# Row normalization on one core: the last scale of the first tile is shared between ScalarE and VectorE

## The chip, the cores and the metric

The kernel runs on one core of a Trainium2 chip. The metric is the device time of one execution in microseconds (us); lower is better. The engines that matter here are VectorE (DVE in the profile), ScalarE (ACT), SyncE (SP), which issues the transfers, and the core's sixteen DMA engines, which carry them out. TensorE does nothing.

## The reference

Each of 1024 rows of 4096 fp32 numbers is divided by its Euclidean norm.

```python
def reference(x, axis, eps):            # x: 1024 x 4096, fp32; axis -1; eps 1e-12
    norm = np.sqrt(np.sum(x ** 2, axis=axis, keepdims=True) + eps)
    return (x / norm).astype(np.float32)
```

So 16.78 MB are read and 16.78 MB are written, and each element is squared, summed and scaled once.

## The kernel before

The 1024 rows are cut into two tiles of 512 rows. A tile (`xt`, one `RowGroups` object each) has 128 partitions with R = 4 consecutive rows each, that is 128 x 4 x 4096 fp32 or 8.39 MB, and lies in SBUF whole; both tiles have a buffer of their own. A tile is loaded by one transfer (line 192) and stored by one (line 213), both issued on the SP queue. Both loads are issued ahead of everything else, the first of them moved to the very front of the program. The two stores follow on the same queue, each as soon as all four rows of its tile are scaled. A helper at the end rearranges the closing barrier; the change doesn't touch it.

What is done to a row r of a tile:

- a square with a running sum into `ssq[:, r]`, on ScalarE (`square_act`, line 33) or on VectorE (`square_dve`, line 42); the squares themselves go to a scratch tile that nobody reads
- `norm`: a square root of the sum on ScalarE (line 53), then its reciprocal on VectorE (line 59), into `rstd[:, r]`
- a multiplication of the row by `rstd[:, r]`, in place: on VectorE (`scale`, line 64) or on ScalarE (`scale_act`, line 69)

The order within a tile is written out by hand in the loop at line 197. VectorE squares row 3 while ScalarE squares row 0; VectorE then scales rows 0, 1 and 3 while ScalarE squares rows 1 and 2. Row 2 is the last one whose sum is ready. In the first tile ScalarE scales it (`scale_act`), in the second tile VectorE does (`scale`). Each engine executes its instructions in the order in which they are written; the waits between engines are put in by the framework from what each instruction reads and writes. The store of a tile waits for the scales of all four rows, on both engines.

Of the kernel before, what the change touches and what calls it, by code (L numbers as in the profile page):

```python
# [13 lines left out]
class RowGroups:  # L14
# [50 lines left out]
            out=self.x[:, r], in0=self.x[:, r], scalar1=self.rstd[:, r : r + 1]  # L65
        )

    def scale_act(self, r):
        self.nc.scalar.activation(  # L69
            out=self.x[:, r],  # L70
            in_=self.x[:, r],
            func=ACT_F.Copy,
            scale=self.rstd[:, r : r + 1],
        )


def first_load_to_front(nc, load):

    def move(program):
        blocks = program.main_func.blocks
        entry = blocks[0].instructions
        if any(i.name == load.name for i in entry):
            return
        body = next(
            b.instructions  # L90
            for b in blocks
            if any(i.name == load.name for i in b.instructions)
        )
        at = next(n for n, i in enumerate(body) if i.name == load.name)
        assert not body[at].sync_info.on_wait
        before = next(
            n
            for n, i in enumerate(entry)
            if i.engine == mybir.EngineType.SP and isinstance(i, mybir.InstDrain)
        )  # L100
        entry.insert(before, body.pop(at))

    nc.at_finalize(move)


def one_barrier_behind_last_store(nc, store):

    SP, POOL = mybir.EngineType.SP, mybir.EngineType.Pool

    def waits(i):
        return i.sync_info.on_wait if i.sync_info is not None else []

    def move(program):
        sem = store.sync_info.on_update[0].id
        tail = program.main_func.blocks[-1].instructions  # L120

        def take(which):
            at = next(n for n, i in enumerate(tail) if which(i))
            return tail.pop(at)

        def place(instructions, which):
            at = max(n for n, i in enumerate(tail) if which(i))
            tail[at:at] = instructions

        arrivals = [  # L130
            n
            for n, i in enumerate(tail)
            if i.engine == SP and isinstance(i, mybir.InstDrain)
        ]
        if any(w.id == sem for w in waits(tail[arrivals[-2]])):
            return
        everything = take(
            lambda i: i.engine == SP and any(w.id == sem for w in waits(i))
        )
        place([everything], lambda i: i.engine == SP and isinstance(i, mybir.InstDrain))  # L140
        reset = take(
            lambda i: i.engine == POOL
            and isinstance(i, mybir.InstDrain)
            and i.is_reset_sema
        )
        clear = take(lambda i: i.engine == POOL and isinstance(i, mybir.InstISA))
        place(
            [reset, clear],
            lambda i: i.engine == POOL and isinstance(i, mybir.InstEventSemaphore),
        )  # L150

    nc.at_finalize(move)


@with_exitstack
def kernel(
    ctx: ExitStack,
    tc: tile.TileContext,
    x: bass.AP,
    axis: bass.AP,  # L160
    eps: bass.AP,
    out: bass.AP,
):
    nc = tc.nc
    P = nc.NUM_PARTITIONS

    assert isinstance(axis, int) and axis in (-1, len(x.shape) - 1)
    eps = float(eps)

    x = x.flatten_outer_dims()  # L170
    out_flat = out.flatten_outer_dims()
    N, D = x.shape
    R = 4
    assert N % (P * R) == 0
    n_tiles = N // (P * R)
    x_t = x.rearrange("(t p r) d -> t p (r d)", p=P, r=R)
    out_t = out_flat.rearrange("(t p r) d -> t p (r d)", p=P, r=R)

    io = ctx.enter_context(tc.tile_pool(name="io", bufs=n_tiles))
    scratch_pool = ctx.enter_context(tc.tile_pool(name="scratch", bufs=1))  # L180
    stats = ctx.enter_context(tc.tile_pool(name="stats", bufs=n_tiles))

    eps_t = scratch_pool.tile([P, 1], F32)
    nc.vector.memset(eps_t, eps)  # L184
    sq_act = scratch_pool.tile([P, D], F32)
    sq_dve = scratch_pool.tile([P, D], F32)
    scratch = {"act": sq_act, "dve": sq_dve}

    groups = []
    for i in range(n_tiles):  # L190
        g = RowGroups(nc, io, stats, scratch, D, R, eps_t)
        load = nc.sync.dma_start(out=g.flat(), in_=x_t[i])
        if i == 0:
            first_load_to_front(nc, load.ins)
        groups.append(g)

    for i, g in enumerate(groups):
        g.square_dve(R - 1)
        g.square_act(0)
        g.norm(0)  # L200
        g.scale(0)
        g.square_act(1)
        g.norm(1)
        g.norm(R - 1)
        g.scale(1)
        g.scale(R - 1)
        g.square_act(2)
        g.norm(2)
        if i < n_tiles - 1:
            g.scale_act(2)  # L210
        else:
            g.scale(2)
        store = nc.sync.dma_start(out=out_t[i], in_=g.flat())
    one_barrier_behind_last_store(nc, store.ins)
# [35 lines left out]
```

## Time and profile before

| | |
|---|---|
| median of 5 runs | 82.54 us (82.45 to 82.84) |
| profiled execution: its time | 82.54 us |
| profiled execution: its span in the profile | 80.8 us |
| DMA queue busy, share of 16 engines | 96.8% |
| ScalarE busy | 30.1 us (37%) |
| VectorE busy | 26.2 us (33%) |
| square of a row on ScalarE, 128x4096 | 3.61 us, 6 times |
| square of a row on VectorE, 128x4096 | 4.43 us, 2 times |
| scale of a row on VectorE, 128x4096 | 2.35 us, 7 times |
| scale of a row on ScalarE, 128x4096 | 3.71 us, once |

The span is the time from the first to the last instruction of the program; the execution's time has 1.7 us more around it. "Busy" is the time in which an engine executes an instruction of the program. Transfers are listed in two ways: by their issue on SP, which takes 0.35 us, and by their packets, which the DMA engines move later. A line of the time line reads: start in us, duration in us, engine, line of the kernel, operation, output <- input, shapes, how often, and in brackets the idle time of the engine just before it with what ended that. A line of a window view reads: the window in us and its length, busy time (and number of instructions) of VectorE, ScalarE and GpSimd, the granted clock, the DMA share, and GB/s. In that view a packet's bytes and time are booked whole where the packet starts, so that a short window can show more than the hardware can move; a packet is 65,536 bytes, four rows of one partition.

### The profile page before, as it was taken

The numbers are of one execution on the slowest core, as the hardware profiler recorded it, in microseconds if no ns is written. First come the engines' busy times: TensorE is split into PE (matmuls) and PEld (weight loads), VectorE is DVE, ScalarE is ACT, GpSimd is POOL, SyncE is SP. The second block draws the span as 40 slices with busy tenths as digits, with TensorE's granted clock in tenths as the row PEclk, the third lists the DMA queues.
The fourth block names the chain that finished last, engine by engine and source line by source line (L and its number), as shares of the span: only waits on it lengthen the run. The fifth ranks groups of instructions, "written<-read, shape, count | busy, mean of one in ns | idle before, by whom it ended". The sixth has DMA issues, their size and how long they took to land.

```text
span 80.8 us, 93 instructions
## 1 busy us (share of the span) xinstructions
DVE 26.2 (33%) x20; ACT 30.1 (37%) x23; POOL 0.2 (0%) x4
## 2 busy tenths in 40 slices
DVE  0000000000199599920059986999000000000000
ACT  6000000000199999989459999930000000000000
POOL 0000000000000000000000000000000000000000
DMA  9099999199999199999199993899992999995690
GB/s 487 32 519 519 519 519 454 65 519 519 519 519 454 65 519 519 519 519 454 65 519 519 519 519 162 357 519 519 519 519 97 422 519 519 519 519 227 292 519 0
DMA packets 576, 33.55 MB, mean 416 GB/s; under 512 B 64, under 2 KB 64, under 8 KB 64
## 3 DMA queue, kind: packets, MB, share of 16 engines
q1 hardware_dynamic: 576, 33.55, 96.8%
HBM read 16.78 MB, written 16.78 MB: 416 GB/s over the span
## 4 chain that ended last, share of the span: by engine, by line
DMA 50%; ACT 10%; DVE 9%; issue 0%
DMA xt<-in_x_dram 50%; ACT sq_act L33 9%; DVE xt L64 9%; ACT rstd L53 1%; DVE rstd L59 0%
## 5 line engine op out<-in xcount | busy, mean ns | idle before, releaser
L33 ACT ACTIVATE sq_act<-xt 128x4096 f32<-128x4096 f32 x6 | 21.6, 3608 | 21.9 <-DMA xt<-in_x_dram 21.9
L42 DVE SCALAR_TENSOR_TENSOR sq_dve<-xt 128x4096 f32<-128x4096 f32 x2 | 8.9, 4426 | 26.8 <-DMA xt<-in_x_dram 26.8
L64 DVE TENSOR_SCALAR xt<-xt,rstd 128x4096 f32<-128x4096 f32 x7 | 16.5, 2353 | 0.2
L69 ACT ACTIVATE xt<-xt,rstd 128x4096 f32<-128x4096 f32 x1 | 3.7, 3709 | 0.2 <-DVE rstd L59 0.2
L53 ACT ACTIVATE rstd<-ssq,eps_t 128x1 f32<-128x1 f32 x8 | 2.1, 289 | 0.1
L59 DVE RECIPROCAL rstd<-rstd 128x1 f32<-128x1 f32 x8 | 1.3, 159 | 2.4 <-ACT rstd L53 2.4
L33 ACT ACT_TABLE_LOAD x1 | 1.3, 1283 | 0.8 <-PEq L231 0.8
L53 ACT ACT_TABLE_LOAD x1 | 1.3, 1283 | 0.0
L33 ACT ACTIVATION_READ_ACCUMULATOR sq_act<-xt 128x1 f32 x6 | 1.1, 186 | 0.0
L184 DVE MEMSET eps_t<- 128x1 f32 x1 | 0.1, 59 | 0.8 <-PEq L231 0.8
L42 DVE DVE_READ_ACCUMULATOR sq_dve<-xt 128x1 f32 x2 | 0.2, 82 | 0.0
L231 POOL MEMSET const-uint8-127<- 128x1 uint8 x1 | 0.1, 103 | 0.0
L231 POOL MEMSET const-bfloat16-1.0<- 128x1 bf16 x1 | 0.1, 102 | 0.0
L231 POOL MEMSET const-float32-0.0<- 128x1 f32 x1 | 0.1, 99 | 0.2 <-issue 0.2
L231 POOL MEMSET const-float32-1.0<- 128x1 f32 x1 | 0.1, 99 | 0.0
## 6 DMA issues: line engine op xcount, KB each, us to landing
xt<-in_x_dram SPq DMA_DIRECT2D x2, 31.2
out_dram<-xt SPq DMA_DIRECT2D x2, 22.6
```

Source lines behind the costliest of these rows:

```text
L33: self.nc.scalar.activation(out=sq_a, in_=self.x[:, r], func=ACT_F.Square, accum_out=self.ssq[:, r : r + 1],)
L42: self.nc.vector.scalar_tensor_tensor(out=sq_v, in0=self.x[:, r], scalar=1.0, in1=self.x[:, r], op0=ALU.mult, op1=ALU.mult, accum_out=self ...
L53: self.nc.scalar.activation(out=self.rstd[:, r : r + n], in_=self.ssq[:, r : r + n], func=ACT_F.Sqrt, bias=self.eps_t,)
L59: self.nc.vector.reciprocal(out=self.rstd[:, r : r + n], in_=self.rstd[:, r : r + n])
L64: self.nc.vector.tensor_scalar_mul(out=self.x[:, r], in0=self.x[:, r], scalar1=self.rstd[:, r : r + 1])
L69: self.nc.scalar.activation(out=self.x[:, r], in_=self.x[:, r], func=ACT_F.Copy, scale=self.rstd[:, r : r + 1],)
L184: nc.vector.memset(eps_t, eps)
L231: nc = _bacc.Bacc("TRN2", target_bir_lowering=False, num_devices=1)
```

## The change

In the first tile, the scale of row 2 is cut: columns 0 to 3071 are scaled on ScalarE, columns 3072 to 4095 on VectorE. `scale_act` goes, `scale_by_both` takes its place; VectorE's part is written behind ScalarE's. The second tile is as before.

```diff
-    def scale_act(self, r):
+    def scale_by_both(self, r):
+
+        cut = 3 * self.D // 4
+        rstd = self.rstd[:, r : r + 1]
         self.nc.scalar.activation(
-            out=self.x[:, r],
-            in_=self.x[:, r],
+            out=self.x[:, r, :cut],
+            in_=self.x[:, r, :cut],
             func=ACT_F.Copy,
-            scale=self.rstd[:, r : r + 1],
+            scale=rstd,
+        )
+        self.nc.vector.tensor_scalar_mul(
+            out=self.x[:, r, cut:], in0=self.x[:, r, cut:], scalar1=rstd
         )
...
         g.norm(2)
         if i < n_tiles - 1:
-            g.scale_act(2)
+            g.scale_by_both(2)
         else:
             g.scale(2)
         store = nc.sync.dma_start(out=out_t[i], in_=g.flat())
```

## The prediction, made before the changed kernel was run

> **What bounds the kernel now.** I read the page's slices and queue rows first, because they say whether any compute engine can matter at all.
>
> ```profile
> DVE  0000000000199599920059986999000000000000
> ACT  6000000000199999989459999930000000000000
> DMA  9099999199999199999199993899992999995690
> q1 hardware_dynamic: 576, 33.55, 96.8%
> HBM read 16.78 MB, written 16.78 MB: 416 GB/s over the span
> ```
>
> VectorE and ScalarE are idle for more than half of the span, and the one DMA queue is busy for 96.8% of it on all sixteen engines. The low digits in the DMA row are no pauses: a packet is a block of 64 KB (four rows of 16 KB), booked in the slice in which it starts, so a slice in which no engine happens to start one looks empty. The chain of waits on the page gives DMA 50% and compute 20%, since it follows the last instruction (the second store's issue at 56.6 us) and not the last byte. The transfers themselves end near 79.8 us. So the next view is the time line around the changed instruction, with the queue that carries the store.
>
> ```profile
> 35.29 0.16 DVE L59 RECIPROCAL rstd<-rstd 128x1 f32<-128x1 f32 x1 [0.57 <-ACT rstd L53]
> 35.49 3.71 ACT L69 ACTIVATE xt<-xt,rstd 128x4096 f32<-128x4096 f32 x1 [0.23 <-DVE rstd L59]
> 39.23 0.35 SPq L213 DMA_DIRECT2D out_dram<-xt  x1
> 41.24 3.62 ACT L33 ACTIVATE sq_act<-xt 128x4096 f32<-128x4096 f32 x1 [2.04 <-DMA xt<-in_x_dram]
> 41.24 4.43 DVE L42 SCALAR_TENSOR_TENSOR sq_dve<-xt 128x4096 f32<-128x4096 f32 x1 [5.78 <-DMA xt<-in_x_dram]
> ```
>
> The first store is issued 0.03 us behind the scale on ScalarE (L69), so that scale does set its issue. But the second load, issued near 0.8 us, lands only at 41.2 us: the store is queued behind a transfer that is still running. What the issue time is worth is decided at the hand-over from load to store. I cut it into windows of 0.1 us; the last column is GB/s, and 655 is one packet starting.
>
> ```profile
> 37.90:38.00 0.10, 0.00 (x0) 0.10 (x1) 0.00 (x0) 1.00 1.51 655
> ...
> 38.40:38.50 0.10, 0.00 (x0) 0.10 (x1) 0.00 (x0) 1.00 3.03 1311
> ```
>
> ```profile
> 40.40:40.50 0.10, 0.00 (x0) 0.00 (x0) 0.00 (x0) 1.00 0.01 0
> 40.50:40.60 0.10, 0.00 (x0) 0.00 (x0) 0.00 (x0) 1.00 1.58 656
> 40.60:40.70 0.10, 0.00 (x0) 0.00 (x0) 0.00 (x0) 1.00 1.54 655
> 40.70:40.80 0.10, 0.00 (x0) 0.00 (x0) 0.00 (x0) 1.00 13.83 5898
> 40.80:40.90 0.10, 0.00 (x0) 0.00 (x0) 0.00 (x0) 1.00 3.06 1311
> 40.90:41.00 0.10, 0.00 (x0) 0.00 (x0) 0.00 (x0) 1.00 3.07 1311
> 41.00:41.10 0.10, 0.00 (x0) 0.00 (x0) 0.00 (x0) 1.00 1.53 655
> ```
>
> One packet takes 1.51 x 0.1 us x 16 = 2.42 us. The load's last sixteen packets start from 37.9 to 38.5 us (1, 4, 6, 1, 2 and 2 in the six windows, mean 38.18), so a seamless hand-over would start the store's first sixteen at a mean of 40.60. They start at a mean of 40.79 (1, 1, 9, 2, 2, 1). The gap is 0.19 us per engine. The same windows at the other two hand-overs, from load to load at 21.0 us and from store to store at 60.0 us, show the sixteen starts exactly one packet time after the batch before, with no gap. So 0.2 us is all that an earlier first store could win; the queue is full everywhere else from 1.0 to 79.8 us.
>
> **The change, part by part.** *Removed:* one 128x4096 scale on ScalarE, 3.71 us. *Added:* a 128x3072 scale there. The rows bound it by 0.29 us (a 128x1 activation, L53) and 3.71; it is far nearer to the second, and a straight line between them gives 0.29 + 3.42 x 0.75 = 2.85 us. Beside it, a 128x1024 scale on VectorE, between 0.16 us (128x1, L59) and 2.35 us (128x4096, L64): the line gives 0.16 + 2.19 / 4 = 0.71 us. It needs the reciprocal that VectorE itself has just made, so it runs from about 35.5 to 36.2 us. It is hidden by ScalarE's longer part; without that cover it would cost its 0.71. ScalarE's part runs from 35.49 to 38.34, and the store is issued at about 38.37 instead of 39.23: 0.86 us earlier. ScalarE's squares take 3.60 us beside VectorE's scales and 3.62 alone, so I book no slowing of one by the other.
>
> *Waits.* The store on the SP queue now has two last writers, as it had two engines to wait for before; nothing but the second store stands behind it there. On VectorE the next instruction is the second tile's square, which waits for the load until 41.24 in any case: of its idle 5.78 us, 0.71 is used up. On ScalarE the wait for the second load grows from 2.04 to 2.9 us. That is where the 0.86 us goes: the second load is late next, and nothing downstream moves.
>
> *The hand-over.* The trace does not show what the 0.19 us is. One bound: it is lateness of the store's descriptors. From the issue at 39.23 to the first packet are 1.3 us, and the first load, issued at 0.00, starts its packets from 1.0 to 2.2 us, so the way to the engines takes about that long; 0.86 us earlier would close the gap, 0.19 us won. The other bound: it is what an engine needs to turn from loading to storing, and nothing is won. A loss of the same size has no row behind it except the slower rival below. I take nothing won. If descriptors were late, the engines that finish the load last would not wait, while the first would wait longest. The starts keep the shape of the ends instead: 0.5 to 0.6 us from first to last in both, shifted as a whole, with the first store start about 0.2 after the first load end (37.9 + 2.42 = 40.3 to 40.4, against 40.5 to 40.6) and the last about 0.2 after the last (40.8 to 40.9 against 41.0 to 41.1).
>
> The Trainium skill bears on this spot: its page "DMA: Bandwidth & Descriptors", section "Latency and other measured facts", gives about 600 ns from issue to first byte for a transfer issued from SP. By that figure the store's descriptors stood ready at 39.83, half a microsecond before the first engine was free, the gap would be no lateness, and the sum would stay 82.54; by the 1.3 us of the row it could be 82.35. No row here shows 0.6 us; the trace's shortest is 1.0.
>
> **The sum.** The profiled execution took 82.54 us, which is also the median of the five (82.45 to 82.84); its span is 80.8, with 1.7 around it. Compute on the path to the first store: -0.86. Given back in the wait for the queue: +0.86, less a gain from the hand-over between 0 and 0.19. With 0 taken: 82.54, said as **82.5 us**.
>
> **The rivals.** *A, the gap closes.* The descriptors were late, all sixteen engines pass straight from load to store, and every later packet moves up 0.19 us: the second store, issued at 56.6 us, is 3.4 us ahead of its turn at 60.0 and follows. 82.54 - 0.19 = **82.35 us**. For it: the two late engines (packets started at 38.4 to 38.5) can be matched with the two store starts at 40.8 to 40.9 without a gap, and the 1.0 to 2.2 us of the first load. Against it: the shape above.
>
> *B, slower: the second load lands late.* With store packets right behind it on every engine, the load's completion might be reported only after one of them: 2.42 us. The second tile takes from 41.24 to 56.60, and its store must be issued by 60.0 - 1.35 = 58.65 to keep the queue full, so there are 2.05 us of slack; from there on a late landing costs its excess. 2.42 - 2.05 = 0.37, so **82.9 us**. Against it: at 21.0 us the second load's packets already follow the first's without a gap, and the first tile's squares still start at 21.90, 0.3 to 0.4 us after the last packet ended, as at 41.24.
>
> *C, the sharing doesn't happen.* If VectorE's quarter is made to wait for ScalarE's part of the same row, it ends at 38.34 + 0.2 + 0.71 = 39.25 and the store is issued when it was: **82.54 us**. Against it: engines work on different rows of one tile side by side all through the time line, and the two parts don't overlap.
>
> **How the numbers follow.** The forecast has 0.57, A 0.30, B 0.07, C 0.06. A measurement of this kernel can tell about 0.3%, 0.25 us, from no change. A sits at -0.23%, just inside, so half of its chance falls to either side: 0.15 to faster. The forecast and C give 0.03 to each side by the spread of the runs. Faster 0.18, slower 0.07 + 0.03 = 0.10, within 0.72. The range holds A with the spread below it and most of the way to B: 82.1 to 82.85 us.
>
> **What would show it.** In the changed profile: L69's successor at about 2.85 us and a VectorE scale of 0.7 us beside it at 35.5; the first store's issue at 38.3 to 38.4; the second load still landing at 41.2 and the second tile's squares at 41.24; the first store packets at 40.5 to 41.1 as before. Packets already from 40.3 would be A. Squares later than 41.5 and a second store issued after 58.6 would be B. I am wrong beyond these if the packet time of 2.42 us itself changes, since 32 of them in a row make up 77.4 of the 80.8 us.

## The result, and the profile after

| | before | after |
|---|---|---|
| median of all runs | 82.53 us (82.33 to 82.84, 62 runs) | 82.39 us (82.22 to 82.63, 35 runs) |
| ratio after / before, 95% interval | | 0.9984 (0.9977 to 0.9990) |
| profiled execution: time, span | 82.54, 80.8 us | 82.73, 81.0 us |
| DMA queue busy | 96.8% | 96.6% |

The kernel became 0.14 us faster by the medians: a small gain, but one whose interval does not reach 1. The profiled execution of after, with 82.73 us, is slower than all 35 runs of the table and 0.3 us above their median; below it is used for what happens in it, and not for its length.

The time line of the changed kernel around the shared scale:

```profile
35.31 0.16 DVE L59 RECIPROCAL rstd<-rstd 128x1 f32<-128x1 f32 x1 [0.57 <-ACT rstd L53]
35.51 0.75 DVE L78 TENSOR_SCALAR xt<-xt,rstd 128x1024 f32<-128x1024 f32 x1
35.51 2.86 ACT L72 ACTIVATE xt<-xt,rstd 128x3072 f32<-128x3072 f32 x1 [0.23 <-DVE rstd L59]
38.39 0.35 SPq L219 DMA_DIRECT2D out_dram<-xt  x1
41.70 4.42 DVE L42 SCALAR_TENSOR_TENSOR sq_dve<-xt 128x4096 f32<-128x4096 f32 x1 [5.44 <-DMA xt<-in_x_dram]
41.70 3.62 ACT L33 ACTIVATE sq_act<-xt 128x4096 f32<-128x4096 f32 x1 [3.34 <-DMA xt<-in_x_dram]
```

The two parts start together, VectorE is done long before ScalarE, and the store is issued at 38.39 instead of 39.23 us. The second load lands later than before, 41.7 against 41.2. What became of the 0.84 us shows in the hand-over from load to store. First, how long the load's last packets take. A window that holds exactly the last sixteen of them (1049 GB/s in 1 us is sixteen packets) has their mean duration in us as its DMA share. Before:

```profile
37.70:38.70 1.00, 0.00 (x0) 1.00 (x1) 0.00 (x0) 1.00 2.42 1049
```

After:

```profile
37.70:38.70 1.00, 0.00 (x0) 0.66 (x1) 0.00 (x0) 1.00 2.56 1049
```

Sixteen packets start in both, but after the change each takes 2.56 us in the mean instead of 2.42. Then the starts of the store's first packets after the change, in windows of 0.1 us:

```profile
40.40:40.50 0.10, 0.00 (x0) 0.00 (x0) 0.00 (x0) 1.00 6.07 2622
40.50:40.60 0.10, 0.00 (x0) 0.00 (x0) 0.00 (x0) 1.00 4.55 1966
40.60:40.70 0.10, 0.00 (x0) 0.00 (x0) 0.00 (x0) 1.00 4.55 1966
40.70:40.80 0.10, 0.00 (x0) 0.00 (x0) 0.00 (x0) 1.00 4.56 1966
40.80:40.90 0.10, 0.00 (x0) 0.00 (x0) 0.00 (x0) 1.00 3.03 1311
...
41.30:41.40 0.10, 0.00 (x0) 0.00 (x0) 0.00 (x0) 1.00 1.52 655
```

Fifteen engines start from 40.4 to 40.9 us and one at 41.4; before it was 40.5 to 41.1. By the packet records each start lies 2 to 3 ns behind the end of a load packet. So two things changed at one spot, with opposite signs: the gap of 0.20 us per engine is gone, and the load's last packets are longer, 0.14 us per engine in the mean and 0.47 us on the one that is late. This late engine stays late to the end, and the end of an execution is set by the slowest engine.

A third thing changed behind that spot: the store's own packets are shorter after the change. The windows that hold its first sixteen, before and after (some small packets in them add about 0.01):

```profile
40.30:41.30 1.00, 0.06 (x1) 0.06 (x1) 0.00 (x0) 1.00 2.46 1049
```

```profile
40.40:41.40 1.00, 0.00 (x0) 0.00 (x0) 0.00 (x0) 1.00 2.43 1049
```

By the packet records the sixteen store packets of an engine, in both stores together, take 38.82 us before and 38.69 after: 0.13 us less, 0.10 of it in the first store.

### The profile page after: what moved, and what is told of

Its sections match the earlier page's. It is cut to its first block, busy times and chain, and to the rows that moved or that the text cites. A ratio compares the mean times of both kernels' runs of the same rounds, so it can differ in the third digit from the quotient of the medians.

```text
span 81.0 us, 94 instructions
## 1 busy us (share of the span) xinstructions
DVE 27.0 (33%) x21; ACT 29.3 (36%) x23; POOL 0.2 (0%) x4
## 3 DMA queue, kind: packets, MB, share of 16 engines
q1 hardware_dynamic: 576, 33.55, 96.6%
## 4 chain that ended last, share of the span: by engine, by line
DMA 51%; ACT 10%; DVE 9%; issue 0%
DMA xt<-in_x_dram 51%; ACT sq_act L33 9%; DVE xt L64 9%; ACT rstd L53 1%; DVE rstd L59 0%
## 5 line engine op out<-in xcount | busy, mean ns | idle before, releaser
L72 ACT ACTIVATE xt<-xt,rstd 128x3072 f32<-128x3072 f32 x1 | 2.9, 2857 | 0.2 <-DVE rstd L59 0.2
L78 DVE TENSOR_SCALAR xt<-xt,rstd 128x1024 f32<-128x1024 f32 x1 | 0.8, 752 | 0.0
```

Of the source, the lines that this page charges most:

```text
L72: self.nc.scalar.activation(out=self.x[:, r, :cut], in_=self.x[:, r, :cut], func=ACT_F.Copy, scale=rstd,)
L78: self.nc.vector.tensor_scalar_mul(out=self.x[:, r, cut:], in0=self.x[:, r, cut:], scalar1=rstd)
```

## The experiments

For each run the same three figures were read from the packet records: how many of the sixteen engines paused between load and store, the mean gap, and the mean stretch of the last load packet beyond 2.418 us. The records don't name the engine of a packet; a pause is counted where no load packet ends 2 to 3 ns ahead of the start, so that where most engines pause the count can be too low by some chance matches. The ratios of e1 to e4, of e5 to e8 and of e9 to e12 come from one chip each, with runs of before on the same chip. In the order of the store's issue:

| run | issue, us | engines with a gap | gap, us | stretch, us | ratio to before |
|---|---|---|---|---|---|
| e7 row 2 not scaled | 34.97 | 0 | 0.00 | 1.17 | 1.0104 (1.0085 to 1.0122) |
| e6 cut at 1/2 | 37.41 | 0 | 0.00 | 0.83 | 1.0065 (1.0051 to 1.0080) |
| e3 row on VectorE | 38.02 | 0 | 0.00 | 0.37 | 1.0046 (1.0034 to 1.0059) |
| e9 the change (3/4) | 38.13 | 0 | 0.00 | 0.17 | 0.9997 (0.9983 to 1.0011) |
| e1 the change (3/4) | 38.33 | 0 | 0.00 | 0.06 | 0.9987 (0.9976 to 0.9997) |
| e5 row on VectorE, held back | 38.54 | 0 | 0.00 | 0.04 | 0.9962 (0.9947 to 0.9976) |
| e2 cut at 7/8 | 38.77 | 1 | 0.02 | 0.01 | 0.9973 (0.9961 to 0.9984) |
| e11 cut at 29/32 | 38.82 | 1 | 0.02 | 0.01 | 0.9966 (0.9954 to 0.9978) |
| e10 cut at 15/16 | 38.89 | 2 | 0.03 | 0.01 | 0.9979 (0.9967 to 0.9990) |
| e8 cut at 15/16 | 39.03 | 11 | 0.15 | 0.00 | 0.9959 (0.9944 to 0.9973) |
| before | 39.23 | 15 | 0.20 | 0.01 | 1 |
| e4 held back by 2 us | 41.23 | 16 | 1.64 | 0.00 | 1.0140 (1.0126 to 1.0154) |

The issue time of one and the same kernel moves by some tenths of a us between executions (38.13 to 38.39 for the change), because the first load lands at 21.7 to 21.9 us there and everything before the store counts from it. The three figures belong to one profiled execution each, the ratio to many. The sum of an engine's sixteen store packets divides the runs in the same way as the gap does: 38.69 to 38.71 us from e7 down to e10, but 38.79 in e8, 38.82 before and 38.83 in e4. So a late store costs twice, by the gap and by up to 0.13 us in longer store packets behind it; why these are longer, no run shows.

**e1, the change once more.** No edit.

> The changed kernel once more. Theory L (the store's descriptors came late: an engine starts its first store packet at the later of the end of its last load packet and 1.35 to 1.85 us after the issue): the store's issue at 38.4, no gap between the last load packets and the first store packets, ratio to before 0.9984. Theory S (the single late engine of the first profile, whose last load packet ended at 41.38 instead of 40.86, belongs to the change): the load lands at 41.6 to 41.7 again and the span ends with one engine 0.5 us behind the rest. If it is chance, the load lands at 41.2 and the span is 80.5 to 80.6.

Measured: no gap, eight of sixteen last packets stretched, the load landed at 41.24 and no engine was 0.5 us behind. So the single late engine doesn't belong to every execution of the change; the vanished gap and the stretch came back, the stretch at less than half the size.

**e2, a smaller share for VectorE.**

```diff
-        cut = 3 * self.D // 4
+        cut = 7 * self.D // 8
```

> The cut at 7/8 of the row: ScalarE's part takes 0.29 + 3.42 x 7/8 = 3.28 us, the store is issued at 38.8, halfway between the two kernels. Theory L: descriptors at the engines from 40.15 to 40.65, engines free from 40.35 to 40.85, so the gap is under 0.05 us and the whole gain is there: ratio 0.9984. Rival P (the gain goes in proportion to the advance of the issue): half of it, 0.9992.

Measured: 0.9973, as good as the change or better, with an issue 0.4 us later. Rival P's 0.9992 lies outside the interval and falls: the gain doesn't go in proportion to the advance of the issue.

**e3, the row on VectorE alone.**

```diff
-        if i < n_tiles - 1:
-            g.scale_by_both(2)
-        else:
-            g.scale(2)
+        g.scale(2)
```

> The whole row scaled on VectorE (2.35 us), nothing on ScalarE: the store is issued at 37.9, 0.5 us ahead of the changed kernel. Theory L: the queue has no gap left to close, ratio 0.9984 as the changed kernel. Rival P: 1.35 / 0.84 of the gain, 0.9974. If the late engine comes from an early store, it is late here too.

Measured: 1.0046, slower than before, which neither had expected. The window with the last sixteen load packets:

```profile
37.70:38.70 1.00, 0.30 (x1) 0.00 (x0) 0.00 (x0) 1.00 2.79 1049
```

The mean packet takes 2.79 instead of 2.42 us. All sixteen are longer, by 0.17 to 0.52 us. An earlier store can cost more than the gap it closes.

**e4, the store held back until the queue is empty.** On the kernel before:

```diff
+        half = self.x[:, r, : self.D // 2]
+        self.nc.scalar.activation(out=half, in_=half, func=ACT_F.Copy)
```

> The kernel before, with a copy of half of the row onto itself on ScalarE behind the scale (0.29 + 1.71 = 2.0 us): the store is issued at 41.25, when all load packets are done. Theory L: first store packets from 42.6 to 43.1, mean 1.57 us behind the issue, all of the delay on the path: +2.0 us, ratio 1.024. Theory T (descriptors take at most 1.1 us, the gap of before was the turn from load to store): first store packets from 42.3, mean gap 1.7 to 1.75 instead of 2.2, ratio 1.019.

The store is issued at 41.23 us, behind the last load packet (40.92). Its first packets:

```profile
42.00:42.10 0.10, 0.10 (x1) 0.10 (x1) 0.00 (x0) 1.00 9.20 3932
42.10:42.20 0.10, 0.10 (x1) 0.10 (x1) 0.00 (x0) 1.00 13.82 5898
42.20:42.30 0.10, 0.10 (x1) 0.10 (x1) 0.00 (x0) 1.00 1.53 655
```

All sixteen start 0.85 to 1.0 us behind the start of the issue, which itself takes 0.35 us, and not 1.35 to 1.85. By this figure the kernel before had its descriptors at the engines from 40.1 to 40.2 us, ahead of the first load end at 40.35, and they still paused. If a busy engine gets them as fast as an idle one, which no run shows, the plain form of theory L falls, and descriptors must be there for some time before the engine is free if the pause is to be avoided. As it was written down, with 1.35 us at least from issue to first packet, it falls by this run alone. Theory T's 1.1 us held, but its turn from load to store is no fixed cost, since the earlier issues of the table don't pay it. The ratio of 1.014 is below both expectations. The mean gap grew by 1.44 us, but all engines now start within 0.15 us of each other, so that the last one ends only 1.17 us later than before (81.02 against 79.85 us), which agrees with the measured 1.15.

**e5, is it VectorE or the time of the issue?** As e3, with an instruction behind the scale that changes no value and holds the store back:

```diff
         g.scale(2)
+        if i < n_tiles - 1:
+            quarter = g.x[:, 2, : D // 4]
+            nc.vector.tensor_scalar_mul(out=quarter, in0=quarter, scalar1=1.0)
```

> The last scale of the first tile on VectorE whole, and behind it a quarter of the row multiplied by 1.0 in place (0.75 us), which holds the store back: issue at 38.8 instead of 38.0. Theory W (only the time of the issue against the load's last packets counts: too late leaves a gap of 0.2 us, too early stretches the load's last packets): as the cut at 7/8, no stretch, no gap, ratio 0.9973. Rival D (the row on VectorE, and not the early store, makes the load's tail slow): the stretch of 0.37 us per engine stays, ratio 1.0046.

The time line and the last load packets of this run:

```profile
35.43 2.35 DVE L64 TENSOR_SCALAR xt<-xt,rstd 128x4096 f32<-128x4096 f32 x1
37.82 0.69 DVE L218 TENSOR_SCALAR xt<-xt 128x1024 f32<-128x1024 f32 x1
38.54 0.35 SPq L219 DMA_DIRECT2D out_dram<-xt  x1
```

```profile
37.70:38.70 1.00, 0.78 (x2) 0.00 (x0) 0.00 (x0) 1.00 2.45 1049
```

More work, a store half a microsecond later, and the kernel goes from 1.0046 to 0.9962. Rival D falls: with the row on VectorE in both, the later issue alone takes the stretch from 0.37 to 0.04 us. This is the run that tells the two apart.

**e6 and e7, earlier still.** e6 cuts at one half; e7 has no scale of row 2 in the first tile:

```diff
-        if i < n_tiles - 1:
-            g.scale_by_both(2)
-        else:
+        if i == n_tiles - 1:
             g.scale(2)
```

> The cut at one half: ScalarE 2.0 us, VectorE 1.25 us, issue at 37.55, still earlier than with the row on VectorE alone (38.02). Theory W: the last load packets are stretched by 0.37 us per engine or more, no gap, ratio 1.0046 or above. Rival N (the slow run with the row on VectorE alone was of another cause): no stretch, ratio 0.997 to 0.998.

> Row 2 of the first tile is not scaled, so that part of the output stays the input; the first store is issued at 34.8, when two whole packets per engine of the load are still to start. Theory W1 (an engine that holds the store's descriptors while its last load packet runs lets the store's reads in early, and the load's packet pays): the last batch, from 37.8, is stretched by 0.37 us or more, the batches before it aren't; ratio 1.0046 or above. Theory W2 (the issue itself disturbs the packets in flight 0.8 to 2.5 us later): the stretch stands in the batch from 35.5 and the last batch has none; ratio 1.003 to 1.005. Theory P (earlier is better): 0.995.

The batch before the last and the last batch of load packets in e7, whose store is issued at 34.97:

```profile
35.30:36.30 1.00, 0.17 (x1) 0.18 (x1) 0.00 (x0) 1.00 2.42 1049
37.70:38.70 1.00, 0.00 (x0) 0.00 (x0) 0.00 (x0) 1.00 3.58 1049
```

The sixteen packets from 35.3 on run at full speed, though the store was issued before they started; the last sixteen take 3.58 us. W2 (a disturbance by the issue itself) would have shown in the first line and falls; P falls as well, and N with e6 (3.25 us in the same window). With packets of 64 KB the stretch is a matter of an engine's last packet of loading with store packets queued behind it. With the store issued 2.9 us before the first of these last packets starts, it costs 1.17 us per engine, and the time isn't made up in the store's packets, which take 2.42 us here.

**e8, towards the kernel before.** `cut = 15 * self.D // 16`.

> The cut at 15/16: ScalarE 3.50 us, issue at 39.02, between the cut at 7/8 (38.77, one engine of sixteen with a gap of 0.2 us) and the kernel before (39.23, all or all but one). Theory W: some of the engines have the gap of 0.2 us and the others none, mean 0.05 to 0.15, no stretch; ratio 0.998 to 0.999.

Measured: eleven engines with the gap, none stretched, as expected; but 0.9959 and not 0.998 to 0.999. The last engine ended at 79.59 us, that of before at 79.85, although the mean gap was only 0.05 us smaller: in this execution the gaps fell to the engines that were ahead, and the last start of a store packet came at 40.89 us instead of 41.06. This is one profile: whether the gaps fall like that in most runs, and so whether it explains the ratio, is not shown. The mean gap of a single profile doesn't give the ratio.

**e9 to e11, side by side on one chip.** The change, 15/16 again and `cut = 29 * self.D // 32`.

> The changed kernel beside the finer cuts, on one chip: issue at 38.3 to 38.4, no gap, some of the last load packets stretched (0.05 to 0.15 us per engine in the mean); ratio 0.998 to 0.999, so 0.1 to 0.2% behind the cuts at 15/16 and 29/32 by theory W; by the rival that all three differ by chance of the chip alone, the three agree within 0.1%.

> The cut at 15/16 again, beside the changed kernel: issue at 39.0, gap of 0.2 us on some engines, no stretch; ratio 0.996 to 0.9975.

> The cut at 29/32: ScalarE 3.39 us, issue at 38.89. Theory W: a gap on fewer engines than at 39.03 (11 of 16), no stretch; ratio 0.996 to 0.9975.

Measured: 0.9997, 0.9979 and 0.9966, so the two finer cuts are ahead of the change by 0.2 and 0.3% where all three share the chip and the runs of before. The interval of 29/32 lies wholly below that of the change; that of 15/16 overlaps it. The rival that the three agree within 0.1% falls; the change and 15/16 came out just slower than their stated ranges, and the change's stretch of 0.17 us just larger. The last load packets and the first store packets of 29/32:

```profile
37.70:38.70 1.00, 0.00 (x0) 1.00 (x1) 0.00 (x0) 1.00 2.43 1049
```

```profile
40.30:40.40 0.10, 0.00 (x0) 0.00 (x0) 0.00 (x0) 1.00 4.56 1966
40.40:40.50 0.10, 0.00 (x0) 0.00 (x0) 0.00 (x0) 1.00 9.10 3932
40.50:40.60 0.10, 0.00 (x0) 0.00 (x0) 0.00 (x0) 1.00 1.52 655
40.60:40.70 0.10, 0.00 (x0) 0.00 (x0) 0.00 (x0) 1.00 6.08 2622
40.70:40.80 0.10, 0.00 (x0) 0.00 (x0) 0.00 (x0) 1.00 3.03 1311
```

Next to nothing of either cost is there: 2.43 us per packet, and all sixteen starts lie in 40.3 to 40.8, 0.2 us ahead of before. On this chip the version is faster than both kernels: 0.9966 (0.9954 to 0.9978).

**e12, a smaller last packet.** As e3, with the second load in two transfers:

```diff
-        load = nc.sync.dma_start(out=g.flat(), in_=x_t[i])
         if i == 0:
+            load = nc.sync.dma_start(out=g.flat(), in_=x_t[i])
             first_load_to_front(nc, load.ins)
+        else:
+            c = (R - 1) * D
+            nc.sync.dma_start(out=g.flat()[:, :c], in_=x_t[i][:, :c])
+            nc.sync.dma_start(out=g.flat()[:, c:], in_=x_t[i][:, c:])
```

> The row scaled on VectorE alone (issue at 38.0, where the stretch was 0.37 us per engine), and the second tile loaded by two transfers, rows 0 to 2 and then row 3, so that the last load packet of an engine has 16 KB (0.6 us) instead of 64 KB. Theory W1a (the stretch is a share of the packet during which the store's descriptors are there; at most half of it again, as the 1.17 of 2.42 us with the store issued at 35.0): at most 0.3 us per engine, ratio under 1.001. Theory W1b (the stretch is the head of a 64 KB store packet that is read ahead, whatever load packet it meets): 0.37 to 1.2 us, ratio 1.0046 or above.

The store is issued at 37.84. Three windows of this run, with five, six and seven packets of 16 KB starting in them:

```profile
36.00:36.20 0.20, 0.20 (x1) 0.00 (x0) 0.00 (x0) 1.00 0.95 410
...
39.40:39.60 0.20, 0.00 (x0) 0.20 (x1) 0.00 (x0) 1.00 1.65 492
...
40.20:40.40 0.20, 0.00 (x0) 0.20 (x2) 0.00 (x0) 1.00 1.51 573
```

A packet takes 0.95 x 0.2 x 16 / 5 = 0.61 us in the first, 1.65 x 0.2 x 16 / 6 = 0.88 us in the second and 1.51 x 0.2 x 16 / 7 = 0.69 us in the third. Summed over an engine's packets of 16 KB the stretch is 0.44 us, and the ratio 1.0040 (1.0028 to 1.0052): no help, W1a falls. The stretch isn't a share of the last packet: it begins, faintly, in packets that start at 38.5, is largest in those that start from 39.0 to 39.9, where most engines have another load packet to come, and by 40.2 it is small again. W1b's range held the stretch of 0.44 us, and the ratio falls just short of its 1.0046; what an engine does in that time is not shown by any run.

## Why the prediction was right, and where its steps were not

**The compute side** held number by number. ScalarE's part took 2.86 us (2.85 worked out), VectorE's 0.75 (0.71), the issue came at 38.39 (38.37). One reading behind it was wrong: no square of ScalarE runs alone in the time line of before, since those of 3.62 us, at 21.90 and 41.24, run beside VectorE's squares; that no slowing was booked did no harm here. Compute added nothing downstream. What moved there came from the load: it landed later in the profiled execution, at 41.7, and the second store was issued at 57.06, still ahead of the 58.65 at which that would have begun to cost.

**What the 0.86 us is worth** was rightly looked for at the hand-over. The time of 82.39 us lies 0.1 us from the 82.5 that was said, and the difference to before, 0.16%, is inside the 0.3% that was called no change. It lies closer still to rival A's 82.35. That the number held is in part luck: the sum has 0 for the hand-over, and the runs show a gain and a loss there, neither of them in the sum, that partly offset each other.

**The step that failed** is "I take nothing won". The reading of the shape was good: engines do pause by about 0.2 us each behind their own last load packet, and e4 shows that descriptors can reach them in 0.85 to 1.0 us. The conclusion from it, that an earlier store can't remove the pause, was wrong; so was "0.2 us is all that an earlier first store could win", since the store packets behind the gap are longer too, by 0.13 us per engine. The faster versions gained 0.26 us (e11) and 0.32 us (e5) by their medians. One engine of sixteen pauses with the issue at 38.8, none in the runs from 38.1 to 38.5. Rival A has the mechanism, the gap closes; its account of it, that descriptors take 1.3 us and more, was read from busy engines and is not what idle ones show.

**The term that was missing** stands in the sentence "A loss of the same size has no row behind it except the slower rival below". The stretch of the load's last packets is such a loss: 0.06 to 0.17 us per engine in the three profiles of the change, against a gap of 0.20 that closed and 0.13 in the store packets. A's ratio of 0.9977 stands at the very end of the measured interval; e11's ratio, with almost no stretch, lies past it. These are means over engines in single profiles, so the 0.14 us can't be summed up from them exactly. No hand-over in the trace of before could show the stretch, since its one store behind a load came too late to cause it; at the other two hand-overs, load to load and store to store, the successors are queued long ahead without any stretch, and the prediction used the first of them against rival B.

**Rival B** was right that a store close behind a load can hold the load up, and wrong in how it would cost. It was priced through the second tile's slack of 2.05 us; what happens is that the load's packets take longer and everything behind them in the queue moves, from the first tenth on. **Rival C** is out: the parts ran side by side.

## What to carry to other kernels

Where one queue is full from end to end, as here, look at its hand-overs packet by packet before pricing a shorter instruction, and at the packets behind them too. On this queue, which passes from loads to stores, the first store could be issued too late and too early; the best issues were 1.5 to 2.0 us ahead of the mean end of the load (40.5 us), a few tenths later than the change has it. When "earlier" helps, try also a little later and much earlier: one run on each side showed what the change itself could not.

## What was not expected of the hardware

- With a store queued long ahead (issue at 35.0), an engine's last 64 KB load packet took 3.58 us in the mean instead of 2.42. A load queued behind a load and a store behind a store showed nothing of the kind, at 21.0 and 60.0 us.
- From the issue of a store to its first packets were 0.85 to 1.0 us on idle engines; yet engines that became free 1.1 to 1.6 us behind the issue (kernel before) paused by 0.2 us.
- Behind a store that came late (before, e8 and e4) an engine's sixteen store packets took 38.79 to 38.83 us together, against 38.69 to 38.71 in the other runs of the table.
- What decides inside the DMA engine is open; no run here looks inside. The runs show when the pause and the stretch come, and not what the engine does in that time.
